# A hybrid Fourier and state-space layer on one core: the backward half of y and the C-B products are made earlier and kept in DRAM

## The chip, the cores and the metric

The kernel runs as one program on one core of a Trainium2 chip. The metric is the device time of an execution in microseconds; the time of a kernel is the median over its runs. In the text PE is TensorE, DVE is VectorE, ACT is ScalarE, POOL is GpSimd and SP is SyncE, whose queue issues every transfer of this kernel.

## What is computed

One layer of a mixer over 2048 latent tokens of width 1024, with a prefix of 256 context tokens. A combined projection feeds two groups: a Fourier group (512 channels) and an SSD group of 24 heads of 64 channels, four groups of six heads that share B and C of 128 states. The SSD group is scanned in both directions over chunks of 128 tokens; the latent scans start from the state that the context left. The part that the change is about, cut to its core:

```python
xbc = depthwise_conv_grid(xbc, conv_w, conv_b, rows, cols)     # SiLU inside; x, B and C
# per direction, per chunk c, group g, head r (ssd_chunked):
cb = einsum('bclgn,bcsgn->bgcls', cc, bc)                      # C-B product of a chunk, 128x128
y_diag = einsum('bgcls,bgrcls,bcsgrp->bclgrp', cb, lmat, xc)
states = einsum('bcsgn,bgrcs,bcsgrp->bcgrpn', bc, decay_states, xc)
new_state = decay * old_state + states                         # chunk after chunk
y_off = einsum('bclgn,bcgrpn,bgrcl->bclgrp', cc, prev_states, exp(a_cum))
# both directions, then
y = y_f + flip(y_b) + d_skip * xs
out = gated_rmsnorm(y * silu(zs))
```

The layer ends with the output projection, the residual and a final RMSNorm. All of it is in fp32. Products that need more than a single fp32r pass are made from a high part and a low part of each operand, in three matmuls (high x high, high x low, low x high); `split` makes the two parts, the high one by an ACT copy and the low one by a subtraction on DVE or POOL.

## The kernel before

The program is one list of stages. The framework orders the instructions of each engine when it builds the program, from a simulated timeline, with the order of the program text as priority; on the chip that order is fixed, and an instruction waits for its semaphores.

- **Up to 230 us**: adaLN, the norm of x, the projection of the Fourier channels.
- **conv** (230 to 765 us): 20 tiles of 128 channels (12 of x, 4 of B, 4 of C) in the order `CONV_ORDER`. For a tile PE projects four blocks of 512 tokens, ACT copies them into a padded image `img` (two buffers), and `finish` makes half an image at a time: one tap on ACT (L431), eight on DVE (L434) into `acc` (two buffers), then SiLU by ACT into `so` (L438). x and B tiles are transposed on PE in `to_tokens` (L414) and stored as `xtok_d` and `btok_d`; B and C are also stored untransposed in `bcT_d`, and C in two parts in `chl_d`. x and B tiles have the 256 context tokens beside it.
- **dt** (765 to 866 us): softplus of dt, cumulative sums, decays; `sml` holds the factors for the scan (ready with L546 of the second half), `sm_d`, `cum_d` and `q_d` keep others in DRAM. Two PE tiles of projections lie beside it.
- **scan** (870 to 1062 us): the context in both directions and the latent chunks 15 to 1 backwards. `scan_prep` loads x and B of a chunk, splits B (ACT, POOL), weighs x (POOL, L641) and splits it (ACT, DVE). `scan_mm`, four times a chunk, makes three matmuls and the new state from the old (L671 decay, L673 sum, both DVE) in the next of two buffers `hs`. The state before each chunk is stored in `hb_d`. Beside it runs the projection of zs, 40 blocks of 24 matmuls; `interleave(main, side, lead, speed)` mixes the two lists, here with a lead of 95 (scan work comes after the first 95 us of the main list by its written costs) and twice the even pace.
- **Fourier** (1065 to 1215 us): the rest of the Fourier group, and the last 12 blocks of zs. Its tables lie where the tiles of dt and scan were.
- **last stage** (1215 us to the end): 64 units, chunk by chunk forwards, four groups each, in six steps that overlap. `s1` makes the C-B product (L948), copies it, takes its diagonal (L953), makes `dsc` (L957: diagonal times backward dt, plus d_skip) and the decay matrix (L965 to L970). `s2` loads the state `hb` of the backward scan and makes y_off of both directions: `split` of `hf` (low part on DVE) and of `hb` (low part on POOL), three matmuls each (L1005 to L1007), a product with the decays (L1009), the term `xd` (six ACT instructions, L1012) and two sums on POOL (L1013, L1014). `s3` carries the forward state on, with a split of B on the spot. `s4` to `s6` are the diagonal part, the gated norm and the output projection (24 matmuls of 512 columns, L1105 to L1107).

Of the kernel before, what the change touches and what calls it, by code (L numbers as in the profile page):

```python
# [33 lines left out]
CONV_ORDER = [16, 0, 1, 2, 12, 17, 3, 4, 5, 13, 18, 6, 7, 8, 14, 19, 15, 9, 10, 11]  # L34
# [15 lines left out]
def mixer_layer(ctx: ExitStack, tc: tile.TileContext, A: dict, out: bass.AP, taps=None):  # L50
# [32 lines left out]
    btok_d = scratch("btok_d", [NALL, P, 4 * P])  # L83
    chl_d = scratch("chl_d", [NCH, P, G, 2, P], F32R)
    bcT_d = scratch("bcT_d", [NCH, P, G, 2, P])
# [5 lines left out]
    hb_d = scratch("hb_d", [NCH, P, DS])  # L91
# [21 lines left out]
    sc = const.tile([P, KT, 2], F32, name="sc")  # L113

# [281 lines left out]
    with ExitStack() as pc_:  # L396
# [14 lines left out]
        def to_tokens(src, ntile, dst):  # L411
# [5 lines left out]
            store(dst, tk[:, :ntile])  # L417

        def conv_tile(n, ci):
# [8 lines left out]
            def finish(half):  # L428
                r0 = 16 * half
                acc = cp.tile([P, 16, GRID_W], F32, name="acc", tag="acc")  # L430
# [5 lines left out]
                so = cp.tile([P, 8, P], F32, name="so", tag="so")  # L436
                sof = so[:].rearrange("p a b -> p (a b)")
                nc.scalar.activation(sof, acc[:].rearrange("p a b -> p (a b)"), AF.Silu, bias=convb[:, ci:ci + 1])  # L438
                c0 = 8 * half
                if kind == "x" or kind == "B":  # L440
                    dd = xtok_d if kind == "x" else btok_d
                    for q in range(2):
                        to_tokens(sof[:, 512 * q:512 * q + 512], 4,
                                  dd[c0 + 4 * q:c0 + 4 * q + 4, :, j * P:(j + 1) * P].rearrange("c p w -> p c w"))
                if kind != "x":
                    store(bcT_d[c0:c0 + 8, :, j, 0 if kind == "B" else 1, :].rearrange("c p w -> p c w"), so)
                if kind == "C":
                    parts = [cp.tile([P, 8, P], F32R, name=nm, tag=nm, bufs=1) for nm in ("sh", "sl")]
                    split(parts[0], parts[1], so, nc.gpsimd)
                    for i in range(2):  # L450
                        store(chl_d[c0:c0 + 8, :, j, i, :].rearrange("c p w -> p c w").bitcast(F32),
                              parts[i][:].bitcast(F32))
# [19 lines left out]
            so = cp.tile([P, CTX], F32, name="soc", tag="soc")  # L472
# [11 lines left out]
    ssdw = const_tile("ssdw", hfp)  # L484
    pp_ = ctx.enter_context(ExitStack())
    pers = pool("pers", stack=pp_)
    sml = pers.tile([P, NALL, 2, W2], F32, name="sml")

    zf_tile(2)
    pre1 = preload(LNEXP)  # L490
# [776 lines left out]
```

## Time and profile before

| | us |
|---|---|
| median of 3 runs | 1980.51 (1978.22 to 1981.74) |
| the profiled execution, its own time | 1983.29 |
| its span, first to last instruction | 1981.4 |
| PE busy | 1848.8 (93%) |
| DVE busy | 1447.8 (73%) |
| ACT busy | 882.0 (45%) |
| POOL busy | 822.4 (42%) |
| DMA traffic | 253.75 MB, 128 GB/s on average |

The mean granted TensorE clock is 0.972 of full speed. How to read the views: busy time is the time in which an engine has an instruction running, and a matmul's end is modelled, so PE's share is high wherever matmuls follow each other. In a row of a tile stand the line, the engine, what is written and read, the count, the shortest, median and longest duration in ns, and the first and last start. A row of waits names who waited for whom, the total, the times and the longest. The chain of waits goes back from the last instruction, at each step to what released it.

### The profile page before, as it was taken

The numbers are of one execution on the slowest core, as the hardware profiler recorded it, in microseconds if no ns is written. First come the engines' busy times: TensorE is split into PE (matmuls) and PEld (weight loads), VectorE is DVE, ScalarE is ACT, GpSimd is POOL, SyncE is SP. The second block draws the span as 40 slices with busy tenths as digits, with TensorE's granted clock in tenths as the row PEclk, the third lists the DMA queues.
The fourth block names the chain that finished last, engine by engine and source line by source line (L and its number), as shares of the span: only waits on it lengthen the run. The fifth ranks groups of instructions, "written<-read, shape, count | busy, mean of one in ns | idle before, by whom it ended". The sixth has DMA issues, their size and how long they took to land.

```text
span 1981.4 us, 27052 instructions
## 1 busy us (share of the span) xinstructions
PE 1848.8 (93%) x9136; PEld 1510.2 (76%) x9136; DVE 1447.8 (73%) x2082; ACT 882.0 (45%) x2008; POOL 822.4 (42%) x635
## 2 busy tenths in 40 slices
PE   6999999999999999999889997889989999899997
PEld 2799988878888888888767786767777777677775
DVE  3742398998988986329995137988988887888873
ACT  2631144344444443443233335655555555555553
POOL 1321021111101110136662226777777767776742
PEclk8999999999999999999999998899999999999998
DMA  7332132322423423356777456543343343333320
GB/s 265 142 95 77 34 107 66 106 88 74 115 59 91 128 62 111 110 167 233 251 261 261 149 179 196 177 135 116 111 122 108 113 122 120 113 108 116 114 89 36
DMA packets 233468, 253.75 MB, mean 128 GB/s; under 512 B 23313, under 2 KB 194417, under 8 KB 232818
## 3 DMA queue, kind: packets, MB, share of 16 engines
q1 hardware_dynamic: 233330, 252.03, 41.0%
q8 instruction: 73, 1.20, 0.3%
q14 instruction: 65, 0.53, 0.1%
HBM read 165.94 MB, written 86.02 MB: 127 GB/s over the span
## 4 chain that ended last, share of the span: by engine, by line
PE 54%; DVE 30%; DMA 5%; ACT 4%; issue 4%; POOL 1%; SPq 1%; DVEq 0%; ACTq 0%; POOLq 0%
DVE acc L434 10%; PE pj L170 8%; PE pj L169 8%; PE pj L171 8%; PE po L1105 4%; PE po L1106 4%; PE po L1107 4%; DMA hb_d<-hs 2%; DVE w L970 2%; DVE xl L72 2%; PE pj L381 2%; PE pj L380 2%; PE pj L379 2%; PE py L1046 1%; DVE hs L671 1%
## 5 line engine op out<-in xcount | busy, mean ns | idle before, releaser
L434 DVE SCALAR_TENSOR_TENSOR acc<-img,c_convw,acc 128x1024 f32<-128x1024 f32 x320 | 464.2, 1458 | 58.8 <-ACT acc L431 48.9
L170 PE MATMUL pj<-hl,wh 128*128 128x512 f32 x1152 | 453.2, 393 | 0.0
L169 PE MATMUL pj<-hh,wh 128*128 128x512 f32 x1152 | 452.0, 396 | 1.2 <-DVE hs L673 1.2
L171 PE MATMUL pj<-hh,wl 128*128 128x512 f32 x1152 | 452.4, 393 | 0.0
L72 POOL TENSOR_TENSOR wl<-raw,wh 128x1024 fp32r<-128x1024 f32 x48 | 122.3, 2548 | 591.5 <-ACT wh L68 568.0
L171 PEld LDWEIGHTS pj<-hh,wl 128*128 128x128 f32 x1152 | 217.3, 189 | 45.1 <-issue 0.2
L169 PEld LDWEIGHTS pj<-hh,wh 128*128 128x128 f32 x1152 | 218.2, 189 | 43.7 <-DVE hs L673 1.5
L170 PEld LDWEIGHTS pj<-hl,wh 128*128 128x128 f32 x1152 | 217.7, 189 | 42.0 <-issue 1.8
L1105 PE MATMUL po<-hl,mh 128*128 128x512 f32 x384 | 160.1, 417 | 21.2 <-ACT mh L68 19.7
L1106 PE MATMUL po<-hh,mh 128*128 128x512 f32 x384 | 155.2, 404 | 0.4 <-DVE hh L729 0.4
L1107 PE MATMUL po<-hl,ml 128*128 128x512 f32 x384 | 146.1, 403 | 0.6 <-POOL ml L72 0.6
L1012 ACT ACTIVATE xd<-xg,dsc 128x64 f32<-128x64 f32 x384 | 98.7, 336 | 36.9 <-DVE dsc L957 34.1
L965 PE MATMUL parg<-rt,lt 128*128 128x384 f32 x256 | 96.8, 390 | 17.1 <-DVE parg L967 10.9
L1105 PEld LDWEIGHTS po<-hl,mh 128*128 128x128 f32 x384 | 74.2, 193 | 42.8 <-ACT mh L68 25.8
L438 ACT ACTIVATE so<-acc,c_convb 128x1024 f32<-128x1024 f32 x40 | 46.1, 1153 | 129.9 <-DVE acc L434 129.9
L72 POOL TENSOR_TENSOR ml<-gt,mh 128x384 fp32r<-128x384 f32 x64 | 68.4, 1069 | 84.4 <-ACT mh L68 81.9
L1013 POOL TENSOR_TENSOR us<-us,xd 128x384 f32<-128x384 f32 x64 | 66.1, 1033 | 77.9 <-ACT xd L1012 77.7
L68 ACT ACTIVATE mh<-gt 128x384 fp32r<-128x384 f32 x64 | 33.4, 522 | 120.2 <-DVE gt L1071 117.1
L72 POOL TENSOR_TENSOR sl<-hb,sh 128x384 fp32r<-128x384 f32 x64 | 81.5, 1273 | 11.9 <-ACT sh L68 11.8
L641 POOL TENSOR_TENSOR xt<-xt,sml 128x768 f32<-128x768 f32 x38 | 66.9, 1780 | 46.7 <-DMA xt<-xtok_d 24.6
L1106 PEld LDWEIGHTS po<-hh,mh 128*128 128x128 f32 x384 | 74.3, 194 | 14.7 <-DVE hh L729 0.9
L1107 PEld LDWEIGHTS po<-hl,ml 128*128 128x128 f32 x384 | 71.7, 191 | 17.9 <-POOL ml L72 4.3
(390 smaller groups left out, 4158.7 us busy)
## 6 DMA issues: line engine op xcount, KB each, us to landing
raw<-in_win SPq DMA_DIRECT2D x48, 512.0 KB
xt<-xtok_d SPq DMA_DIRECT2D x19, 768.0 KB
xtok_d<-tk SPq DMA_DIRECT2D x48, 256.0 KB
zsT_d<-ev SPq DMA_DIRECT2D x48, 256.0 KB
hb_d<-hs SPq DMA_DIRECT2D x16, 768.0 KB
hb<-hb_d SPq DMA_DIRECT2D x64, 192.0 KB
zs<-zsT_d SPq DMA_DIRECT2D x64, 192.0 KB
xg<-xtok_d SPq DMA_DIRECT2D x64, 192.0 KB
```

The costliest lines, as they stand in the source:

```text
L72: (lo_engine or nc.vector).tensor_tensor(out=lo, in0=src, in1=hi.bitcast(F32), op=ALU.subtract)
L169: mm(po, wh[:, k], a, start=(k == 0), stop=False)
L170: mm(po, wh[:, k], b, start=False, stop=False)
L171: mm(po, wl[:, k], a, start=False, stop=(k == KT - 1))
L434: nc.vector.scalar_tensor_tensor(out=acc, in0=im[:, r0 + dy:r0 + dy + 16, dx:dx + GRID_W], scalar=tap(t), in1=acc, op0=ALU.mult, op1=ALU.add)
L641: nc.gpsimd.tensor_tensor(out=xq, in0=xq, in1=wd, op=ALU.mult)
L965: mm(po, l[:, dr], r[:, cols], start=True, stop=True)
L1012: nc.scalar.activation(xd[:, h], xg[:, h], AF.Copy, scale=d["dsc"][:, h:h + 1])
L1013: nc.gpsimd.tensor_tensor(out=us, in0=us, in1=xd, op=ALU.add)
L1105: mm(po, a, wh[:, i], start=(g == 0 and q == 0), stop=False)
L1106: mm(po, a, wl[:, i], start=False, stop=False)
L1107: mm(po, b, wh[:, i], start=False, stop=(g == 3 and q == 3))
```

## The change

1. **conv**: SiLU is made in place in `acc` (`so` and `soc` go; C has its own two buffers `cacc`). B is split in two parts once, after its transposition (high part ACT, low part POOL), and stored as `bhl_d` in place of `btok_d`. The 64 C-B products are made here (`cb_products`) from C's and B's halves and stored in `cb_d`; `bcT_d` goes. Their diagonals `cbd` come from a product with the identity on POOL and a reduction on DVE. In `CONV_ORDER` each B tile comes right behind its C tile.
2. **dt**: `ecb` (backward exp of the cumulative sums) and `dsc` for all chunks.
3. **scan**: works by single groups instead of chunks. `scan_off` makes the backward y_off, adds `xd` and stores the sum in `yb_d`, in place of the state `hb_d`. The state is kept in place (`hbk`, `hf`); its decay moves from DVE to POOL. x is weighed into a tile of its own. The list has no lead and runs at the even pace; loads run two units ahead.
4. **last stage**: loads `cb`, `yb` and the split B; the C-B product, its copy and diagonal, `dsc`, the backward y_off, `xd`, one of the two POOL sums and the split of B go. The low part of `hf` moves from DVE to POOL.

The diff, cut to its core:

```diff
-CONV_ORDER = [16, 0, 1, 2, 12, 17, 3, 4, 5, 13, 18, 6, 7, 8, 14, 19, 15, 9, 10, 11]
+CONV_ORDER = [16, 12, 0, 1, 2, 17, 13, 3, 4, 5, 18, 14, 6, 7, 8, 19, 15, 9, 10, 11]
...
+        def hl_store(dst, parts, c0, n, j):
+            for i in range(2):
+                store(dst[c0:c0 + n, :, j, i, :].rearrange("c p w -> p c w").bitcast(F32),
+                      parts[i][:, :n].bitcast(F32))
+
+        def b_tokens(src, j, c0, n):
+            parts = hl_tiles()
+            for q in range(0, n, 4):
+                m = min(4, n - q)
+                split(*(t[:, q:q + m] for t in parts), to_tokens(src[:, P * q:P * (q + m)], m), nc.gpsimd)
+            hl_store(bhl_d, parts, c0, n, j)
+
+        def cb_products(bt, ct, j, c0):
+            for q in range(0, 8, 4):
+                pt = tr_psum([P, 4, P])
+                for i in range(q, q + 4):
+                    mm(pt[:, i - q], bt[:, i * P:(i + 1) * P], ct[:, i * P:(i + 1) * P], start=True, stop=True)
+                tk = cp.tile([P, 4, P], F32, name="tk", tag="tk")
+                copy(tk, pt)
+                store(cb_d[c0 + q:c0 + q + 4, :, j, :].rearrange("c p w -> p c w"), tk)
+                dg = cp.tile([P, 4, P], F32, name="dg", tag="dg", bufs=1)
+                nc.gpsimd.tensor_tensor(out=dg, in0=tk, in1=ident[:].unsqueeze(1).broadcast_to([P, 4, P]), op=ALU.mult)
+                nc.vector.tensor_reduce(out=cbd[:, c0 + q:c0 + q + 4, j], in_=dg, axis=AX.X, op=ALU.add)
...
-                acc = cp.tile([P, 16, GRID_W], F32, name="acc", tag="acc")
+                acc = cp.tile([P, 16, GRID_W], F32, name="acc", tag="cacc" if kind == "C" else "acc")
...
-                nc.scalar.activation(sof, acc[:].rearrange("p a b -> p (a b)"), AF.Silu, bias=convb[:, ci:ci + 1])
+                nc.scalar.activation(sof, sof, AF.Silu, bias=convb[:, ci:ci + 1])
...
+                elif kind == "B":
+                    b_tokens(sof, j, c0, 8)
+                    cb_products(sof, cso[half], j, c0)
...
+            nc.gpsimd.tensor_copy(out=ecb[:, cl], in_=ecum[:, :nl, H:])
+            dv = dsc[:, cl]
+            nc.vector.tensor_tensor(out=dv, in0=dtt[:, :nl, H:]..., in1=cbd[:, cl]..., op=ALU.mult)
+            nc.vector.tensor_tensor(out=dv, in0=dv, in1=dsk[:]..., op=ALU.add)
...
+        def scan_prep(dr, c, g):
             def go():
+                gs = slice(g * GW, (g + 1) * GW)
+                d = st[dr, c, g] = {}
+                xt = d["x"] = sp.tile([P, HG, 64], F32, name="xt3", tag="xt", bufs=4)
+                load(xt[:].rearrange("p h w -> p (h w)"), xtok_d[c, :, gs])
+                if dr == 1 and c < NCH:
+                    d["c"] = sp.tile([P, 2, P], F32R, name="cc3", tag="cc", bufs=3)
+                    load(d["c"][:].bitcast(F32), chl_d[c, :, g].bitcast(F32))
+                if (dr, c) == (1, 0):
+                    return
+                d["b"] = sp.tile([P, 2, P], F32R, name="bb3", tag="bb", bufs=3)
+                load(d["b"][:].bitcast(F32), bhl_d[c, :, g].bitcast(F32))
+                xw = sp.tile([P, HG, 64], F32, name="xw3", tag="xw")
...
+                nc.gpsimd.tensor_tensor(out=xw, in0=xt, in1=wd, op=ALU.mult)
+                d["xh"], d["xl"] = (sp.tile([P, GW], F32R, name=t + "3", tag=t, bufs=3) for t in ("xh", "xl"))
+                split(d["xh"], d["xl"], xw[:].rearrange("p h w -> p (h w)"))
...
+        def scan_off(c, g):
+            def go():
+                gs = slice(g * GW, (g + 1) * GW)
+                d = st[1, c, g]
+                sh, sl = (sp.tile([P, GW], F32R, name=t + "3", tag=t) for t in ("sh", "sl"))
+                split(sh, sl, hbk[:, gs])
+                po = main_psum()[:, :GW]
+                mm(po, d["c"][:, 0], sh, start=True, stop=False)
+                mm(po, d["c"][:, 0], sl, start=False, stop=False)
+                mm(po, d["c"][:, 1], sh, start=False, stop=True)
+                yb, xd = (sp.tile([P, HG, 64], F32, name=t, tag=t) for t in ("yb3", "xd3"))
+                for h in range(HG):
+                    nc.scalar.activation(xd[:, h], d["x"][:, h], AF.Copy, scale=dsc[:, c, g, h:h + 1])
+                ec = ecb[:, c, g * HG:(g + 1) * HG].unsqueeze(2).broadcast_to([P, HG, 64])
+                nc.vector.tensor_tensor(out=yb, in0=po.rearrange("p (h w) -> p h w", w=64), in1=ec, op=ALU.mult)
+                nc.gpsimd.tensor_tensor(out=yb, in0=yb, in1=xd, op=ALU.add)
+                store(yb_d[c, :, gs], yb[:].rearrange("p h w -> p (h w)"))
...
+        def scan_mm(dr, c, g):
...
+                nc.gpsimd.tensor_tensor(out=h3, in0=h3, in1=dec, op=ALU.mult)
+                nc.vector.tensor_tensor(out=hv, in0=hv, in1=pst, op=ALU.add)
...
-        interleave(zs_ops([(7, range(4))] + [(i, (0, 1, 2)) for i in range(8, 20)]), side, 95, 2, True)
+        interleave(zs_ops([(7, range(4))] + [(i, (0, 1, 2)) for i in range(8, 20)]), side, 0, 1, True)
...
-            split(sh, sl, hsrc, (nc.vector, nc.gpsimd)[dr])
...
-        nc.gpsimd.tensor_tensor(out=us, in0=us, in1=xd, op=ALU.add)
-        nc.gpsimd.tensor_tensor(out=ts, in0=ts, in1=us, op=ALU.add)
+        split(sh, sl, hf[:, gs], nc.gpsimd)
+        mm(po, d["chl"][:, 0], sh, start=True, stop=False)
+        mm(po, d["chl"][:, 0], sl, start=False, stop=False)
+        mm(po, d["chl"][:, 1], sh, start=False, stop=True)
+        ec = d["sml"][:, 2, g * HG:(g + 1) * HG].unsqueeze(2).broadcast_to([P, HG, 64])
+        nc.vector.tensor_tensor(out=ts, in0=po, in1=ec, op=ALU.mult)
+        nc.gpsimd.tensor_tensor(out=ts, in0=ts, in1=yb, op=ALU.add)
...
-        bh, bl = (wa.tile([P, P], F32R, name=t, tag=t, bufs=1) for t in ("bh4", "bl4"))
-        split(bh, bl, d["b"], nc.vector)
+        bh, bl = d["b"][:, 0], d["b"][:, 1]
```

178 lines of the change are left out of this document (71 added, 107 removed).

## The prediction

> **What bounds the kernel now.** I read the busy times by stage first, then the chain of waits stage by stage, then single tiles. The stages (columns: stretch, its length, then PE, weight loads, DVE, ACT and POOL busy, clock, DMA share, GB/s) are conv, scan and the last stage with its 64 units; dt and Fourier lie between:
>
> ```profile
> 230.00:765.00 535.00, 526.67 (x2625) 444.69 (x2624) 475.16 (x354) 221.87 (x315) 70.31 (x28) 0.99 0.30 87
> ...
> 866.00:1065.00 199.00, 182.98 (x818) 152.00 (x817) 166.35 (x200) 63.31 (x90) 120.52 (x65) 0.97 0.71 238
> ...
> 1215.00:1982.00 767.00, 684.94 (x3569) 540.53 (x3567) 628.62 (x1210) 422.30 (x1292) 523.70 (x470) 0.95 0.38 116
> ```
>
> PE looks full everywhere, but matmuls overlap in the record, so this alone is no bound. DVE is busy for 89% of conv, 84% of the scan and 82% of the last stage. The chain of waits for conv, the scan and most of the last stage (the view cuts its long line):
>
> ```profile
> by line: DVE acc L434 35.9%; PE pj L169 16.5%; PE pj L170 16.5%; PE pj L171 16.4%; PE ptr L414 4.5%; ACT so L438 1.7%; PE pc L170 1.6%; PE pc L169 1.6%; PE pc L171 1.6%; ACT acc L431 1.1%; issue 0.8%; DVE accc L470 0.6%; ACT img L68 0.6%; A
> ...
> by line: DMA hb_d<-hs 17.5%; DVE xl L72 16.2%; DVE hs L671 14.7%; DVE hs L673 9.4%; DVE gate L686 8.1%; issue 7.7%; PE pj L170 6.1%; PE pj L171 6.0%; PE pj L169 5.9%; DVE hs L668 1.7%; DVE hf L671 1.1%; PE ptr L689 1.0%; DVE hf L673 0.8%; P
> ...
> by line: PE po L1105 11.1%; PE po L1106 10.6%; PE po L1107 10.5%; issue 6.4%; DVE w L970 4.5%; PE py L1046 3.9%; DVE parg L967 3.8%; DVE sl L72 3.1%; DVE rs L1069 3.0%; DVE bl L72 3.0%; ACT xd L1012 2.9%; DVE gt L1071 2.7%; DVE hf L1037 2.5
> ```
>
> Conv is shared between PE and the DVE taps, so both are near critical. The scan hangs on DVE and on a store. The last stage is a mixture in which PE has a third. Next, single tiles (min/median/max ns), and one collision, out of the chain and out of POOL's timeline:
>
> ```profile
> L434 DVE SCALAR_TENSOR_TENSOR acc<-img,c_convw,acc x320: 1270/1285/3506, 238.4 to 763.4; 128x1024 f32<-128x1024 f32 x160
> L72 POOL TENSOR_TENSOR wl<-raw,wh x48: 2366/2540/3117, 21.4 to 1169.8; 128x1024 fp32r<-128x1024 f32 x48
> L1009 DVE TENSOR_TENSOR us<-pyo,sml x64: 537/545/559, 1217.0 to 1926.3; 128x384 f32<-128x384 f32 x64
> L72 DVE TENSOR_TENSOR sl<-hf,sh x64: 541/549/2451, 1205.7 to 1913.7; 128x384 fp32r<-128x384 f32 x64
> L72 POOL TENSOR_TENSOR sl<-hb,sh x64: 988/1250/1742, 1208.8 to 1917.8; 128x384 fp32r<-128x384 f32 x64
> ...
> 398.33 3.35 DVE acc L434
> ...
> 398.19 2.40 POOL L72 TENSOR_TENSOR sl<-so,sh 128x1024 fp32r<-128x1024 f32 x1 [10.10 <-ACT sh L68]
> ```
>
> POOL runs from 398.19 to 400.59; the tap started beside it ends at 401.68, 1.09 us after POOL, where it needs 1.27 alone. So the two took turns but for 0.18 us. A DVE split with two SBUF inputs (sl from hf) ranges from 541 to 2451 ns, while a product with a PSUM input (us) stays within 537 to 559 in the same stage, beside the same POOL work. I therefore add POOL's instructions and DVE's two-SBUF-input instructions into one sum, called the shared path, and take 0.18 us off each DVE one.
>
> The Trainium skill, page "SBUF — State Buffer", section "SBUF: two separate sides", says that the pair of ports shared by VectorE and GpSimd is locked for the whole instruction and that the loser blocks fully. The collision above agrees but for its 0.18 us; what whole durations would make of the scan is rival (4).
>
> **The conv stage.** Prices of what it gets:
>
> ```profile
> L1056 DVE TENSOR_REDUCE s<-sq x64: 579/598/608, 1229.5 to 1956.3; 128x128 f32<-128x384 f32 x64
> DVE acc L434 <- ACT acc L431: 48.9, 17, 6.8
> ...
> 1512.84 0.49 PE L948 MATMUL pcb<-bc 128*128 128x128 f32 x2
> 1513.16 0.38 PE L1049 MATMUL py<-c_ident,ts 128*128 128x128 f32 x2
> ```
>
> The split of B adds 16 low parts of 512 columns and 4 of 256 on POOL (sl of hb takes 0.99 for 384, so 1.32 and 0.66: 24 us), with as many ACT copies. The C-B products add 64 matmuls (0.32 us to the next start, 20 us), 16 ACT copies, 16 POOL products with the identity (21 us) and 16 DVE reductions (0.58 for 384 columns, so 0.77: 12 us). Stores of bcT and btok go, those of bhl and cb come: 36 on SP become 40, at nothing, since the stage moves 87 GB/s. ACT is busy 222 of 535 us and hides its copies. So DVE gets 12 us, and behind 45 us of POOL work up to 40 us of turns, 52 in all; PE gets 20. The lower end is 14, if DVE stays covered by PE and a product costs a third less; the upper is 60, if DVE also stands before a reduction until POOL's identity product is done, with the next taps behind it. The waits for L431 (48.9 us) show that DVE has little reserve, but only 4 of the 20 tiles carry the load and img has two buffers. I take **+38**, nearer to DVE's price. SiLU in place keeps an acc buffer until its transposes are done; its next user comes a half tile, some 13 us, later, so nothing. If that cover is gone, L431 waits on ACT with DVE behind it. ecb and dsc are six small operations in the dt stage, where DVE is mostly idle: 0.
>
> **The scan stage.** Its start, end and prices:
>
> ```profile
> 852.94 0.61 DVE L546 TENSOR_TENSOR sml<-sml,smx 128x432 f32<-128x432 f32 x1
> L673 DVE TENSOR_TENSOR hs<-hs,ptr x32: 536/541/555, 915.6 to 1062.1; 128x384 f32<-128x384 f32 x32
> L641 POOL TENSOR_TENSOR xt<-xt,sml x38: 1468/1786/2191, 870.1 to 1044.9; 128x768 f32<-128x768 f32 x38
> L72 POOL TENSOR_TENSOR bl<-bt,bh x19: 1289/1641/2008, 873.0 to 1051.5; 128x512 fp32r<-128x512 f32 x19
> L72 DVE TENSOR_TENSOR xl<-xt,xh x38: 942/1122/3161, 872.5 to 1055.1; 128x768 fp32r<-128x768 f32 x38
> L671 DVE TENSOR_TENSOR hs<-hs,sml x64: 543/558/2233, 905.0 to 1058.9; 128x384 f32<-128x384 f32 x64
> L686 DVE SCALAR_TENSOR_TENSOR gate<-ev,sc,gate x16: 736/1307/2469, 891.1 to 1042.9; 128x512 f32<-128x512 f32 x16
> L1025 POOL TENSOR_TENSOR xw<-xg,sml x60: 823/836/1550, 1207.7 to 1879.1; 128x384 f32<-128x384 f32 x60
> L1036 POOL TENSOR_TENSOR hf<-hf,sml x60: 822/872/1547, 1209.8 to 1875.1; 128x384 f32<-128x384 f32 x60
> L1013 POOL TENSOR_TENSOR us<-us,xd x64: 996/1012/1726, 1219.7 to 1942.5; 128x384 f32<-128x384 f32 x64
> L1012 ACT ACTIVATE xd<-xg,dsc 128x64 f32<-128x64 f32 x384 | 98.7, 336 | 36.9 <-DVE dsc L957 34.1 <-DMA lt<-q_d 0.8 <-POOL xl L72 0.7
> L63 SPq DMA_DIRECT2D hb_d<-hs x16: 319/320/539, 924.5 to 1062.7; - x16
> ```
>
> Before, 870 to 1062, by minima: on POOL xt 38 x 1.468, bl 19 x 1.289 and about 8 wl x 2.37; on DVE xl 38 x 0.942, the decay of hs and hf 68 x 0.543, gate 16 x 0.736: 184 us. Less 122 x 0.18 this is 162 us on the shared path in 192, 0.84 full.
>
> After: on POOL xw 76 x 0.823, the decay 68 x 0.822, yb plus xd 64 x 0.996, wl 19: 201 us; on DVE xl 76 x 0.541, sl 64 x 0.541, gate 12: 88. That is 289, less 156 x 0.18: 261 us. The yb products and the state sums read PSUM and run beside it. At 0.84 full the scan takes 311 us, wholly full 261. The hb_d store, 17.5% of the stage's chain (35 us of 199), goes, and without it 162 us would have filled all of 157; so I take a value between, 0.92: 284 us. Beside it lie ACT (99 us of xd and 64 sh splits on top of 63) and PE. SP gets 276 transfers (76 xt, 72 B, 64 C, 64 yb) instead of 54, at 0.32 us 71 us more of issuing within 284: hidden. The wait that is added is SP's for POOL before each yb store; behind it stand the loads two units on and the next weights. The start is set by sml (ready at 853.6): without the lead 856 instead of 870. The end is 1140 instead of 1062: **+78** (+55 to +105). The Fourier stage follows, because its tables lie where sml and the scan's tiles were; PE, free for part of the scan, may do a few of its zs blocks early: **-10** (0 to -50).
>
> **The last stage.** Its period and PE's spacing:
>
> ```profile
> L1052 DVE SCALAR_TENSOR_TENSOR gt<-py,zs x64: 537/545/559, 1226.9 to 1955.1; 128x384 f32<-128x384 f32 x64
> 1506.21 0.34 PE L1005 MATMUL pyo<-sh,chl 128*128 128x384 f32 x1
> 1506.39 0.34 PE L1006 MATMUL pyo<-sl,chl 128*128 128x384 f32 x1
> 1508.08 0.39 PE L1105 MATMUL po<-hl,mh 128*128 128x512 f32 x1
> 1508.32 0.39 PE L1106 MATMUL po<-hh,mh 128*128 128x512 f32 x1
> ```
>
> A unit takes (1955.1-1226.9)/63 = 11.56 us. Out of it go PE's pcb and three pyo (0.32 + 3 x 0.18 = 0.86), DVE's us, dsc, diagonal and bl, ACT's cb, bh, one sh and six xd, POOL's sum of us and xd (1.0). The split sl of hf moves from DVE to POOL, where it takes the place of that of hb. PE's large matmuls need 24 x 0.24 + 13 x 0.18 = 8.1 us; with the small ones, about one us (estimated from pcb), 9.1 now and 8.2 after. In the chain above sl, bl and xd have 9.0% of the time, and us, dsc, the diagonal, pcb and pyo, by their lengths, some 6% more: 15% off gives 9.8 us. The shared path loses POOL's 1.0 and most of DVE's three splits, which shortens the turns of w, rs and gt: I take 9.6, so 1.95 x 63 = **-123**. The ends are 10.5 (PE as full as now, 8.2 of 10.5), -65, and 9.1 (PE 90% full), -155. SP issues as many loads a unit as before: 0.
>
> Sum: +38+78-10-123 = -17 on the profiled execution's 1983.3 (span 1981.4), 1966; the median of the runs is 2.8 lower, so 1964.
>
> **The rivals.** (1) Slower: SP stands before each yb store, the loads two units on come late, and a unit of the scan loses 0.67 us: 51 more, 2015. For it: stores already hold 17.5% of that chain. Against: a slice is a quarter of hb_d's. It decides once the scan takes over 301 us. (2) PE uses its free time in the scan for most of the 12 zs blocks of the Fourier stage (24 x 0.24 each, 69 us): 40 us more off, 1924. Against: the order on an engine is fixed at build. (3) The last stage waits as it does now and gains 65: 2022. (4) Work is moved and not saved: the shared path counts whole durations, 289 us at the 184/192 of before, so 302, end 1158, 18 more: 1982, no change. Against: the 0.18 us above.
>
> **How the numbers follow.** Forecast 0.44 (its own range 1935 to 2000), (1) 0.25, (2) 0.14, (3) 0.10, (4) 0.07. The range reaches from (2) past (1) and (3), 1918 to 2028, which leaves out some 2 in 10 of their spread. Within 0.2% (4 us), about what a measurement of this kernel can tell from no change, lie a part of the forecast and most of (4): 0.10. Faster is three quarters of the forecast and (2), 0.47; slower 0.43.
>
> **What would show it.** gt's period near 9.6 us; a scan from 856 to 1140 with POOL busy for three quarters of it; DVE near 520 us busy in conv, where it was 475; the decay of the backward state gone from DVE's rows. The forecast is wrong if the scan ends later than 17 us past its 1140 beyond conv's shift, or if gt's period stays above 10.

## The result and the profile after

The changed kernel takes 1996.16 us (median of 4 runs, 1995.1 to 1998.23) against 1980.09 us for the kernel before: a ratio of 1.0083, 95% interval 1.0065 to 1.0100. It is 0.8% slower, where the forecast was 0.8% faster. The profiled execution took 1995.1 us, its span 1993.2.

The busy times of the changed kernel by stage, in the columns of the prediction's first table (conv, dt, scan, last stage), and behind them dt and scan of the kernel before:

```profile
230.00:802.00 572.00, 544.89 (x2746) 459.56 (x2744) 505.10 (x369) 238.30 (x350) 144.27 (x64) 0.99 0.29 82
802.00:891.00 89.00, 55.19 (x252) 43.08 (x250) 36.20 (x57) 27.02 (x42) 5.94 (x4) 0.79 0.38 109
891.00:1190.00 299.00, 283.66 (x1264) 238.20 (x1264) 202.53 (x294) 189.20 (x572) 230.69 (x220) 0.94 0.72 216
1340.00:1994.00 654.00, 599.58 (x3247) 478.96 (x3247) 498.75 (x834) 286.32 (x721) 448.28 (x410) 0.96 0.45 136
```

```profile
765.00:870.00 105.00, 105.00 (x502) 86.99 (x501) 33.30 (x48) 45.88 (x63) 11.98 (x5) 1.00 0.45 128
870.00:1062.00 192.00, 175.98 (x787) 146.19 (x786) 165.80 (x199) 62.12 (x88) 120.52 (x65) 0.97 0.71 237
```

Two things stand out. In dt TensorE was busy for all of 105 us with 502 matmuls; now it is busy for 55 of 89 us with 252, at a granted clock of 0.79. In the scan it was busy for 176 of 192 us with 787 matmuls; now it has 1264 and is busy for 284 of 299 us. Of the 477 matmuls more, 192 are new there (three of y_off for each of 64 units), and 250 are those that dt no longer has. The stage's engines that the forecast looked at, DVE and POOL, are busy for 0.68 and 0.77 of it.

The single tiles that date the stages in the changed kernel (min/median/max ns, first start to last start; the line numbers are those of the changed kernel):

```profile
L470 DVE SCALAR_TENSOR_TENSOR acc<-img,c_convw,acc x320: 1269/1285/3352, 238.2 to 801.0; 128x1024 f32<-128x1024 f32 x160
L579 DVE TENSOR_TENSOR sml<-sml,smx x2: 607/608/610, 847.7 to 879.6; 128x432 f32<-128x432 f32 x2
L686 POOL TENSOR_TENSOR xw<-xt,sml x76: 822/830/1382, 891.6 to 1161.9; 128x384 f32<-128x384 f32 x76
L725 POOL TENSOR_TENSOR hbk<-hbk,sml x64: 819/832/1156, 909.2 to 1172.9; 128x384 f32<-128x384 f32 x64
L706 POOL TENSOR_TENSOR yb<-yb,xd x64: 1000/1288/1482, 925.3 to 1189.4; 128x384 f32<-128x384 f32 x64
L1088 DVE SCALAR_TENSOR_TENSOR gt<-py,zs x64: 540/550/560, 1353.4 to 1967.2; 128x384 f32<-128x384 f32 x64
L1107 DVE TENSOR_TENSOR gt<-gt,rs x64: 542/884/1539, 1363.4 to 1975.5; 128x384 f32<-128x384 f32 x64
```

Read one below the other with the rows of the kernel before, they give the balance. The last tap starts at 801.0 instead of 763.4 (+37.6). The scan ends with the last sum of yb, 1189.4 and its one us, instead of 1062.6 (+128, so +90 beyond conv). The first gt starts at 1353.4 instead of 1226.9 (+126.5), so the Fourier stage between takes 163 us as it took 164. A unit of the last stage takes (1967.2 - 1353.4) / 63 = 9.74 us instead of 11.56, so the 63 periods between the first and the last gt give back 114 us. The last gt is 12.1 us later than before, and so is the span (+11.8).

The scan starts when x arrives and not when sml is ready, which is at 880.2: SP issues the first load of x at 888.90, behind dt's last stores, and POOL waits for it (the row in POOL's timeline, with its wait in brackets):

```profile
891.63 0.83 POOL L686 TENSOR_TENSOR xw<-xt,sml 128x384 f32<-128x384 f32 x1 [13.33 <-DMA xt<-xtok_d]
```

The chain of waits of the changed kernel, for the scan and for the last stage (the view cuts its long line):

```profile
by line: PE pj L172 17.0%; PE pj L170 16.9%; PE pj L171 16.8%; issue 3.9%; DMA xt<-xtok_d 3.5%; PE ptr L717 3.4%; POOL yb L706 3.3%; PE ptr L716 3.3%; PE ptr L718 3.2%; PE pj L698 2.8%; DMA ev<-in_wada_g 2.8%; POOL xw L686 2.8%; PE pj L699 
...
by line: PE po L1143 14.0%; PE po L1142 13.8%; PE po L1141 13.7%; PE py L1082 5.7%; issue 4.9%; PE parg L1008 4.2%; PE py L1085 3.2%; DMA wo<-in_wout 2.7%; DMA xg<-xtok_d 2.4%; DVE gt L1107 1.8%; PE pn L1098 1.6%; DVE w L1013 1.6%; DVE parg
```

In the kernel before, the scan hung on DVE and a store; now the three matmuls of the zs projection (L170 to L172) hold half of its chain. In the last stage TensorE's output matmuls, the first of the chain before too, went from a third of it to over 41%, and DVE's lines fell behind.

### The profile page after: what moved, and what is told of

Read it like the earlier page. It is cut to its first block, busy times and chain, and to the rows that moved or that the text cites. A ratio compares the mean times of both kernels' runs of the same rounds, so it can differ in the third digit from the quotient of the medians.

```text
span 1993.2 us, 27660 instructions
## 1 busy us (share of the span) xinstructions
PE 1835.8 (92%) x9136; PEld 1507.1 (76%) x9136; DVE 1382.5 (69%) x1820; ACT 868.2 (44%) x1932; POOL 918.8 (46%) x760
## 4 chain that ended last, share of the span: by engine, by line
PE 37%; DVE 7%; DMA 6%; POOL 3%; ACT 2%; issue 2%; SPq 1%; DVEq 0%; ACTq 0%; POOLq 0%
PE po L1143 5%; PE po L1142 5%; PE po L1141 5%; PE pj L170 4%; PE pj L172 4%; PE pj L171 4%; PE py L1082 2%; PE parg L1008 1%; DMA wo<-in_wout 1%; PE py L1085 1%; DMA xg<-xtok_d 1%; PE ptr L849 1%; SPq L63 1%; DVE gt L1107 1%; PE pn L1098 1%
## 5 line engine op out<-in xcount | busy, mean ns | idle before, releaser
L470 DVE SCALAR_TENSOR_TENSOR acc<-img,c_convw,acc 128x1024 f32<-128x1024 f32 x320 | 485.6, 1524 | 49.2 <-ACT acc L467 39.6
L172 PE MATMUL pj<-hh,wl 128*128 128x512 f32 x1152 | 455.4, 395 | 0.0
L170 PE MATMUL pj<-hh,wh 128*128 128x512 f32 x1152 | 453.5, 398 | 0.0
L172 PEld LDWEIGHTS pj<-hh,wl 128*128 128x128 f32 x1152 | 218.5, 190 | 45.9 <-issue 0.5
L170 PEld LDWEIGHTS pj<-hh,wh 128*128 128x128 f32 x1152 | 219.4, 190 | 42.0 <-issue 1.8
L703 ACT ACTIVATE xd<-xt,dsc 128x64 f32<-128x64 f32 x384 | 101.3, 336 | 75.9 <-POOL yb L706 69.8
L473 ACT ACTIVATE acc<-acc,c_convb 128x1024 f32<-128x1024 f32 x40 | 46.1, 1152 | 160.4 <-DVE acc L470 160.4
L1012 ACT ACTIVATE w<-parg 128x384 f32<-128x384 f32 x128 | 62.3, 487 | 110.0 <-DVE parg L1010 109.6
L1013 DVE TENSOR_TENSOR w<-w,cb 128x768 f32<-128x768 f32 x64 | 85.9, 1342 | 13.1 <-ACT w L1012 12.3
L68 ACT ACTIVATE xh<-xw 128x384 fp32r<-128x384 f32 x136 | 70.2, 517 | 56.7 <-POOL xw L686 25.1
L686 POOL TENSOR_TENSOR xw<-xt,sml 128x384 f32<-128x384 f32 x76 | 68.4, 901 | 52.8 <-DVE xl L72 32.5
L1051 POOL TENSOR_TENSOR ts<-ts,yb 128x384 f32<-128x384 f32 x64 | 73.8, 1154 | 40.8 <-issue 18.3
L1010 DVE COPY_PREDICATED parg<-msk,parg 128x384 f32<-128x384 uint8 x128 | 70.8, 553 | 30.3 <-PE parg L1008 30.2
L68 ACT ACTIVATE tk<-ptr 128x512 f32<-128x512 f32 (+1 forms) x96 | 51.3, 556 | 88.7 <-PE ptr L415 50.6
```

The source lines that it names most:

```text
L68: return nc.scalar.activation(dst, src, AF.Copy).ins
L170: mm(po, wh[:, k], a, start=(k == 0), stop=False)
L172: mm(po, wl[:, k], a, start=False, stop=(k == KT - 1))
L470: nc.vector.scalar_tensor_tensor(out=acc, in0=im[:, r0 + dy:r0 + dy + 16, dx:dx + GRID_W], scalar=tap(t), in1=acc, op0=ALU.mult, op1=ALU.add)
L703: nc.scalar.activation(xd[:, h], d["x"][:, h], AF.Copy, scale=dsc[:, c, g, h:h + 1])
L1013: nc.vector.tensor_tensor(out=w, in0=w, in1=cb[:].unsqueeze(1).broadcast_to([P, HG, P]), op=ALU.mult)
```

## The experiments

Two theories stood at first. "PE": the lead before the first scan step (95 us of projection work, removed by the change) kept TensorE busy during dt; without it that work falls into the scan, and TensorE sets the scan's length. "Shared path": the POOL instructions and DVE's two-SBUF-input instructions, taken in turns, set it. Ratios are to the kernel before on the same chip, with 95% intervals; the changed kernel's is 1.0083. Most intervals reach 0.002 to each side, 4 us; the times inside a run come from one profiled execution.

**The lead put back into the changed kernel.**

```
-        interleave(zs_ops(...), side, 0, 1, True)
+        interleave(zs_ops(...), side, 95, 2, True)
```

> The changed kernel with the scan list's lead of 95 and pace of 2 of before. Theory PE (without the lead the scan's steps stand ahead of zs blocks in PE's order while sml is not ready, so PE loses some 42 us in the dt stage, and PE, not the shared path, then sets the scan's end): PE is full again between the end of conv and the scan, the scan of 299 us becomes 255 to 280, the total falls by 25 to 45 us, to 1951 to 1971. Theory shared path (POOL and DVE's two-input instructions set the scan's length, as in the prediction): the scan starts some 15 us later and stays 285 to 300 long; total 1996 to 2010.

Measured: 1996.78 us, 1.0084 (1.0064 to 1.0105), no change, as "shared path" expected. The sums of yb run from 961.7 to 1193.8 and the weighting starts at 909.1: the scan takes 286 us instead of 299, but starts 17 us later. "PE" alone, which expected 1951 to 1971, is refuted.

**A lead of 60 at a pace of 1.45.**

```
-        interleave(zs_ops(...), side, 0, 1, True)
+        interleave(zs_ops(...), side, 60, 1.45, True)
```

> The changed kernel with a lead of 60 and a pace of 1.45: just the zs blocks that fit beside the dt stage come first. Theory PE: as good as the lead of 95 or better by up to 10 us, since the scan's work is spread over more zs blocks; 1945 to 1970. Theory shared path: 1990 to 2000, as the changed kernel.

Measured: 1990.8 us, 1.0060 (1.0039 to 1.0080); the time is what "shared path" expected, the interval overlaps that of the changed kernel, and the profiled execution, at 1983.62 us, was the shortest of six. From 802 to 912 us TensorE now does 486 matmuls, where it did 252 in dt. The scan runs from 912.2 to 1180.9, 269 us. Its tile row, and one window of it beside the same window of the changed kernel (in this order):

```profile
L706 POOL TENSOR_TENSOR yb<-yb,xd x64: 989/1322/1468, 944.6 to 1179.9; 128x384 f32<-128x384 f32 x64
```

```profile
1100.00:1150.00 50.00, 45.63 (x207) 36.80 (x206) 42.12 (x57) 35.12 (x113) 44.26 (x43) 1.00 0.75 231
```

```profile
1100.00:1150.00 50.00, 50.00 (x235) 42.74 (x234) 33.60 (x49) 33.84 (x104) 39.58 (x36) 1.00 0.73 222
```

With this lead TensorE has 207 matmuls in 50 us and room, while DVE and POOL go from 33.6 and 39.6 us to 42.1 and 44.3: the limit has passed from TensorE to the shared path. Summed as in the prediction, by minima (yb's adds 64 x 0.99, and the rest as above), the path holds some 260 us of work in these 269 (0.97 full), and 268 in the changed kernel's 299 (0.90; three more low parts of weights fall into it).

**The lead taken from the kernel before, and its double pace with it.**

```
-        interleave(zs_ops(...), side, 95, 2, True)
+        interleave(zs_ops(...), side, 0, 1, True)
```

> The kernel before with no lead and the even pace (0, 1), nothing else. Theory PE: the same loss without the rest of the change: PE's need fills only some 0.6 of the dt stage instead of all of it, some 20 us of the 40 lost are made up by PE's slack in the scan (0.89 full), total 1990 to 2010. Theory shared path: the scan can start earlier and runs at its own length, total 1970 to 1980.

Measured: 2035.67 us, 1.0276 (1.0253 to 1.0299), the largest effect of all runs, and larger than expected. Its dt and scan, by window, and the last state sums:

```profile
764.00:845.00 81.00, 33.00 (x132) 23.93 (x131) 33.01 (x50) 20.26 (x35) 7.54 (x5) 0.62 0.35 104
845.00:1110.00 265.00, 259.60 (x1177) 219.06 (x1176) 173.30 (x199) 74.71 (x106) 120.77 (x66) 0.99 0.59 192
```

```profile
L673 DVE TENSOR_TENSOR hs<-hs,ptr x32: 537/546/555, 888.8 to 1109.9; 128x384 f32<-128x384 f32 x32
```

The scan starts some 30 us earlier (xt at 839.8 instead of 870.1) and ends 48 us later. TensorE is busy for 33 of 81 us in dt, and then for 98% of the scan with 1177 matmuls in place of 787. So in a kernel whose scan has room on the shared path, the lead and its pace together are worth 56 us, and the early start does not make up for them.

**More buffers for the stores of yb.** This was rival (1).

```
-                yb, xd = (sp.tile(..., tag=t) for t in ("yb3", "xd3"))
+                yb, xd = (sp.tile(..., tag=t, bufs=4) for t in ("yb3", "xd3"))
```

> The changed kernel with four buffers for yb and xd in the scan instead of two. Rival (1) of the prediction (stores of yb, and SP standing before them, set the pace): the scan gets 15 to 50 us shorter. Theory PE and theory shared path: within 5 us of the changed kernel, although ACT's 70 us of waits of xd for POOL's yb shrink.

Measured: 1997.56 us, 1.0084 (1.0057 to 1.0111). The buffers make no difference that shows.

**The sum of yb moved off POOL.** The product stays in PSUM, and DVE adds xd from there.

```
-                nc.vector.tensor_tensor(out=yb, in0=po..., in1=ec, op=ALU.mult)
-                nc.gpsimd.tensor_tensor(out=yb, in0=yb, in1=xd, op=ALU.add)
+                p3 = po.rearrange(...)
+                nc.vector.tensor_tensor(out=p3, in0=p3, in1=ec, op=ALU.mult)
+                nc.vector.tensor_tensor(out=yb, in0=p3, in1=xd, op=ALU.add)
```

> In the scan the sum of the two halves of the backward y is moved from POOL (64 adds of 1182 ns) to DVE: the product stays in PSUM and DVE adds the other half from there. The lead stays 0. Theory 'two limits': in the changed kernel both the path that POOL and DVE share (254 us of work in 299) and PE (271 us) are near the scan's length; taking some 48 us from the path leaves PE as the limit, so the scan shortens only to 280-288 us and the time is 1980 to 1987 us. Theory 'path alone': 206 us of work at 0.85 give a scan of 242 us and a time of 1936 to 1945 us. Theory 'PE alone': no change, 1992 to 1998 us.

Measured: 1990.91 us, 1.0045 (1.0027 to 1.0063): between "two limits" (1980 to 1987) and "PE alone" (1992 to 1998), nearer to the second, and far from "path alone". The scan runs from 893.0 to 1185.5, 292 us; "two limits" expected 280 to 288. POOL is now busy for half of each window and TensorE for nearly all of it, so TensorE held the scan, and the path gave little:

```profile
1050.00:1100.00 50.00, 50.00 (x237) 43.29 (x236) 35.31 (x64) 33.26 (x104) 24.71 (x26) 1.00 0.74 227
```

**The sum of yb on DVE, and the lead of 60.**

> As the run before this one (the add on DVE from PSUM), and with the lead of 60 us and speed 1.45 as in the run with lead 60. Theory 'two limits': PE has then 215 us of work left for the scan and the path 200 us; at 0.9 to 0.95 the scan takes 226 to 240 us instead of 269, and the time is 1948 to 1962 us, so that the two edits together bring far more than the sum of each alone (6 and 12 us). Theory 'path alone': the same as the run with lead 0 but for the start, 1936 to 1945 us in both. Theory 'PE alone': as lead 60 by itself, 1986 to 1992 us.

Measured: 1984.81 us, 1.0011 (0.9994 to 1.0029). All three expectations miss, "PE alone" by only a microsecond: the scan still takes 266 us (912.2 to 1178.3), though TensorE and POOL have room: between 1000 and 1150 TensorE is busy for at most 45.9 of 50 us, POOL for 28.6. The waits of this run between 920 and 1170 name a third limit (who waited for whom: us in total, times, longest):

```profile
POOL xw L686 <- DMA xt<-xtok_d: 50.1, 35, 4.3
ACT xh L68 <- POOL xw L686: 42.9, 40, 3.8
```

POOL's weighting waits for x out of DRAM. In the changed kernel the same wait, over the same window, is a tenth of it:

```profile
POOL xw L686 <- DMA xt<-xtok_d: 5.8, 5, 2.6
```

There, it seems, the other two limits hold everything back first; the next runs test this.

**Loads four units ahead, with both edits above, and two more buffers each for x, B and C.**

```
+        FAR = 4
...
+            if n + FAR < len(seq):
+                side.append((0.0, scan_load(*seq[n + FAR])))
```

> The run with the add on DVE and lead 60, and the scan's loads (x, C, B) issued four units ahead of their use in place of two, with two more buffers each; the weighting and split still two ahead. In that run POOL's weighting waited 50 us for x in 35 places. Theory 'loads': SP issues in order, so the loads stand behind the stores of y that wait for their product, and two units ahead is too late; four ahead removes most of the 50 us, the scan takes 225 to 245 us in place of 266, and the time is 1945 to 1965 us. Rival 'bandwidth': the queues move 227 GB/s at 0.74 to 0.8 of the DMA engines' time and can't bring x sooner however early it is asked for; the scan keeps 260 to 270 us and the time is 1980 to 1988 us.

Measured: 1967.67 us, 0.9935 (0.9914 to 0.9955): faster than both kernels. The wait for x falls, and the scan ends 18 us earlier, after 248 us:

```profile
POOL xw L694 <- DMA xt<-xtok_d: 10.7, 6, 2.3
```

```profile
L715 DVE TENSOR_TENSOR yb<-pj,xd x64: 540/546/559, 944.6 to 1159.7; 128x384 f32<-128x384 f32 x64
```

So x was asked for too late rather than moved too slowly: between 1000 and 1150 the queues now bring 246 to 259 GB/s, where they brought 212 to 249. The scan of 248 us and the time are 3 us above what "loads" expected, and 12 below "bandwidth".

**Earlier loads alone.**

> The changed kernel with the scan's loads issued four units ahead and nothing else. Theory 'several limits': PE is busy 50 of 50 us in each window from 1000 on, so earlier loads alone bring at most 5 us: 1990 to 1998 us. Rival 'loads alone': the scan of the changed kernel is late because of its loads, and it gains 15 to 30 us: 1966 to 1981 us.

Measured: 1992.72 us, 1.0051 (1.0028 to 1.0074). The scan ends at 1187.9 instead of 1190.4. As "several limits" expected, the loads alone bring little.

**Earlier loads and the lead, with the sum on POOL.**

> The changed kernel with lead 60 (speed 1.45) and loads four units ahead; the add of the backward y stays on POOL. It completes the set of three edits. Theory 'three limits, each hiding the others': with PE and the loads relieved, the shared path with its 248 us of work is what is left, at 0.92 to 0.95 full 261 to 269 us of scan, 1982 to 1990 us. Rival 'the add does not matter': the scan is as short as with all three edits (248 us), 1966 to 1973 us.

Measured: 1986.26 us, 1.0028 (1.0010 to 1.0046); the scan runs from 913.7 to 1182.5, 269 us, inside what "three limits" expected. From the run with all three edits (1967.67 us) it differs in the place of the sum alone, and that is worth 21 us of scan. The shared path is what is left, and it is nearly full again:

```profile
1100.00:1150.00 50.00, 47.07 (x214) 39.44 (x213) 43.15 (x57) 34.81 (x111) 47.14 (x43) 0.97 0.76 231
```

POOL is busy for 47 of 50 us. The ends of the scan, side by side, show how the three edits hide each other: none 1190.4; loads 1187.9; sum on DVE 1185.5; lead 1180.9; lead and loads 1182.5; lead and sum 1178.3; all three 1160.3. Single edits bring 3 to 10 us, all three 30; the sum with earlier loads and no lead was not run. How fine are these figures? In the changed kernel and four other runs whose scan is the same but for buffers, the last sum of yb starts 387.2 to 389.2 us after the last tap of conv. Counted so, the loads alone bring 2 us, hardly outside that spread, the sum 5, the lead 8 and all three 29. By this measure the three together clearly bring more than the sum of the single edits, 15. By the ratios of whole times they bring 6, 8 and 5 alone and 29 together, each with some 5 us to either side, which by itself would hardly show it.

**Half of the change: the products, the diagonal and the split of B in conv, the backward half of y in the last stage as before.** States are kept in DRAM and the lead is 95. The edit is shown against the kernel before, cut to its core.

```
-            split(bh, bl, bt, nc.gpsimd)
+            load(b2, bhl_d[c])
...
         scan_mm, the stores of hb_d and the lead as in the kernel before
...
+        load(dsc4, dsc_d[c, :, g])
         both halves of y in s2 as in the kernel before
```

> Half of the change alone: C-B products, their diagonal and the split of B are made in the conv stage and kept in DRAM as in the changed kernel, but the backward half of y stays in the last stage, with the states kept in DRAM, the lead of 95 and the scan's instructions as in the kernel before (less the split of B). Expected: conv +38 as in the changed kernel; scan 182 to 192 us (PE need 171 at 0.9 as before, POOL freed of 32 us of splits); last stage less some 45 us, since 99 us of DVE work leave it (diagonal 17 + 5, its scaling 43, split of B 34) and DVE was busy 610 of 728. Sum 1965 to 1985 us. If the last stage is bound by the path alone (the split of B only, 64 x 0.4), it gains 20 to 28 and the time is 1985 to 1998 us.

Measured: 1973.02 us, 0.9954 (0.9939 to 0.9970), faster than the kernel before.

```profile
L710 DVE TENSOR_TENSOR hs<-hs,ptr x32: 540/544/555, 954.8 to 1098.5; 128x384 f32<-128x384 f32 x32
L1076 DVE SCALAR_TENSOR_TENSOR gt<-py,zs x64: 540/546/558, 1259.8 to 1944.3; 128x384 f32<-128x384 f32 x64
```

The scan ends 36 us later than before, which is conv's growth. A unit takes (1944.3 - 1259.8) / 63 = 10.87 us instead of 11.56, so the last stage gives back 44. Beside the changed kernel this splits the change: the other half, which moves the backward half of y and takes away the lead, puts the first gt 94 us later (1353.4 - 1259.8) and gives back 71 in the last stage (10.87 - 9.74, 63 times). That half loses 23 us, and the half of this run gains 9 (1982.20 - 1973.02). The sum lies inside what was expected.

**Conv: without the diagonal, its factor set to 1.**

```
-                nc.gpsimd.tensor_tensor(out=dg, in0=tk, in1=ident..., op=ALU.mult)
-                nc.vector.tensor_reduce(out=cbd[...], in_=dg, axis=AX.X, op=ALU.add)
```

> The diagonal of the C-B products (16 POOL multiplies and 16 DVE reductions in the conv stage) is left out; the factor that it makes is set to 1, so the backward half of y lacks that factor. All else as in the changed kernel. Theory 'diagonal': the 37 us that the conv stage grew come mostly from these instructions, 11 us of reductions in DVE's queue and some 16 x 1 us in which POOL's multiply keeps DVE's taps waiting, so the last tap ends 20 to 30 us earlier (771 to 781) and the time is 1966 to 1976 us. Rival 'PE order': the growth comes from what stands in PE's queue (64 C-B matmuls, 12 us, and transposes that wait for the split and the copies), so the last tap stays within 6 us of 801 and the time is 1990 to 1997 us.

Measured: 1988.09 us, 1.0032 (1.0016 to 1.0047). The last tap starts at 790.2, 11 us earlier, between the two expectations. That is the length of the 16 reductions (0.68 us each), but the match is partly chance: DVE's 17.0 us of waits for POOL's product also go, and its taps get 7.6 us shorter (444.1 to 436.5), while its waits for ACT's tap grow by 20 us (31.8 to 51.4). The run prices the diagonal as a whole and does not split it.

**Conv: without the diagonal and the C-B products; a slice of C is stored in their place.**

```
-                    mm(pt[:, i - q], bt[...], ct[...], start=True, stop=True)
-                copy(tk, pt)
+                tk = ct[:, q * P:(q + 4) * P]...
```

> As the run without the diagonal, and also without the 64 C-B matmuls and their 16 copies out of PSUM in the conv stage; a slice of C is stored where the product was, so y is another. The run without the diagonal ended conv at 791.5 and took 1988 us. Theory 'PE': the matmuls (12 us of PE's need) and their place in PE's order, behind a Silu, carry the rest, so conv ends at 770 to 783 and the time is 1968 to 1981 us. Rival 'B split': the rest comes from the 20 splits of B on POOL (39 us busy) in turns with DVE's taps; conv ends at 787 to 792 and the time is 1984 to 1991 us.

Measured: 1974.08 us, 0.9960 (0.9940 to 0.9981). The taps of the run without the diagonal and of this one:

```profile
L468 DVE SCALAR_TENSOR_TENSOR acc<-img,c_convw,acc x320: 1268/1285/3437, 237.6 to 790.2; 128x1024 f32<-128x1024 f32 x160
```

```profile
L464 DVE SCALAR_TENSOR_TENSOR acc<-img,c_convw,acc x320: 1270/1285/3349, 237.5 to 778.3; 128x1024 f32<-128x1024 f32 x160
```

Another 12 us go with the 64 matmuls and 16 copies. So conv's 37.6 us are 11 for the diagonal, 12 for the products, and 15 for what is left: the split of B, the SiLU in place and the order of the tiles.

**Conv: the old order of tiles.**

```
-CONV_ORDER = [16, 12, 0, 1, 2, 17, 13, 3, 4, 5, 18, 14, 6, 7, 8, 19, 15, 9, 10, 11]
+CONV_ORDER = [16, 0, 1, 2, 12, 17, 3, 4, 5, 13, 18, 6, 7, 8, 14, 19, 15, 9, 10, 11]
```

> The changed kernel with the conv stage's tiles in the order of the kernel before (each B tile two or three tiles behind its C tile, not right behind it). Theory 'order': two tiles in a row whose products and transposes wait for the same Silu leave PE waiting (51 us of waits of transposes on Silu against 16 before); with the old order the last tap ends 10 to 25 us earlier and the time is 1972 to 1986 us. Rival 'instructions': the growth of conv comes from the added instructions alone and the last tap stays within 5 us of 801: 1991 to 1999 us.

Measured: 1996.72 us, 1.0079 (1.0058 to 1.0099), with the last tap at 796.2, as "instructions" expected. In nine runs with the conv stage of the changed kernel the last tap starts at 799.6 to 801.1, so the order is worth some 3 to 5 us in conv; the whole time does not show it.

> The half of the change that was 0.5% faster than the kernel before (products and split in conv, backward half of y in the last stage), with the conv stage's old order of tiles. If the order costs what 'order' says, 1950 to 1965 us; if it costs nothing, 1970 to 1977 us.

This is the half of the change once more, with the old order of tiles. Measured: 1967.91 us, 0.9923 (0.9898 to 0.9948). The interval overlaps that of the run without the order (0.9939 to 0.9970), so a difference between the two is not shown.

**All edits of the scan, and the old order.**

> The changed kernel with lead 60, the add on DVE from PSUM, loads four units ahead and the conv stage's old order of tiles, which ended conv 4 us earlier. Expected: 4 us less than the run without the order, 1960 to 1968 us, 0.7 to 1.1% under the kernel before.

Measured: 1963.25 us, 0.9901 (0.9873 to 0.9929), the lowest median of all versions, 1% under the kernel before; its interval overlaps those of the run without the order and of the half of the change with it. Conv ends 3 us earlier than in the run without the order, and the scan's sums end at 1156.6 instead of 1160.3.

## Why the prediction was wrong

The sum was -17 us against the kernel before's profiled execution; it came out at +12. No single term carries the difference of 29: three of four were each some 10 us too good.

- **Conv, +38: right, at +37.6, and right in its bounds; its split was not.** The forecast gave DVE 12 us of reductions and up to 40 of turns with POOL, took a value between 14 and 60, and that it met the measured one is luck. DVE's taps took 485.6 us in all instead of 464.2, so the turns that were added came to some 21. The runs show 11 for the diagonal as a whole, and 12 for the C-B products, which stood there as PE's 20. DVE is busy for 505 us, not 520. The 15 us that are left were not taken apart.
- **Scan, +78: +90, and here the failing step lies.** The start came out right by luck: 856 and conv's 38 make 894, and it came at 891.6. But the forecast had it set by sml, which was ready 11 us before, and the first load of x came later than it. The duration was 299 instead of 284. The sentence that failed is "Beside it lie ACT ... and PE", together with the removal of the lead counted as a gain of 14 us in the start alone: TensorE's need in the scan was put at nothing, without a sum. The lead was what let TensorE do 502 matmuls during dt. Without it TensorE did 252 there, carried the rest into the scan, got 192 new ones beside, and was full in it: its 1264 matmuls, at the 235 in 50 us of the full window shown above, need 269 us (an estimate). The run with a lead of 60 has the path at 0.97 full, better than the forecast's 0.92, and a scan of 269; the kernel before without its lead and pace is 56 us slower. The rows for this stood in the profile: 105 of 105 us busy in dt. The forecast's own sign, a scan more than 17 us late beyond conv's shift, was too wide to catch it: the scan was 12 us late.
- **The shared path as the scan's limit: right, but as one of three.** Counted as the forecast counted it, it fits the two runs with a lead of 60 in which POOL keeps the sum, at 269 us in each, and moving the sum shortens the second of them to 248. (With the lead of 95 the sums of yb begin only at 961.7, and the scan takes 286.) Its count was a little off: 12 low parts of weights and 12 gate instructions fell into the scan, not 8 and 16, and SP had 284 transfers there, not 276. The path is why putting the lead back brings 10 us at most: the path is right behind TensorE, and the loads are right behind the path.
- **Rival (1) was half of it.** More buffers for yb change nothing. But loads that were asked for two units ahead did come late once the other limits were lifted, 50 us of waits, and four units ahead only 11.
- **Fourier, -10: -1.** TensorE did nothing early, and rival (2) falls with it. That TensorE was full in the scan is not the whole reason: with the lead of 60 it was busy for 45.6 us of 50, and from the end of the scan to the first gt it still took 162 us (1180.9 to 1342.6). The order fixed at build, which the forecast set against rival (2), fits; no run tests it.
- **Last stage, -123: -114.** The period is 9.74, not 9.6, inside the bound of 10. TensorE's share of its chain has grown, and gt's scaling takes 884 ns in the median where it took 546 in the kernel before; turns of POOL and DVE would explain this, but no run separates them. Rival (3), 65, is far off.
- **Rival (4), whole durations:** its scan of 302 us is near the measured 299, but for another reason. TensorE was busy for 284 of these 299 us, and with the lead of 60 the same kinds of POOL and DVE instructions, 287 us in whole durations, fitted into 269. So each of the 152 DVE instructions among them overlapped POOL's by at least 0.12 us on average; the 0.18 us of the forecast fit that, and were not tested by themselves. The Trainium skill, page "SBUF — State Buffer", section "SBUF: two separate sides", has the shared pair held for the whole instruction. Taken for whole recorded durations, that is not borne out by this kernel.
- **The range** (1918 to 2028) held the time.

## What to carry to other kernels

A lead that fills one engine during another stage is work, not delay: before you price its removal, count what that engine does in the stage (here 502 matmuls in 105 us) and where it will have to do it. Work moved into a stage must be set against each resource of that stage by itself, engines, shared ports and the depth of its loads, because the longest alone shows in the profile, and an edit that lifts one uncovers the next: here three edits brought 3, 5 and 10 us of scan alone and 30 together. And split a change before you judge it: one half of this one was faster than the kernel before, and the other half, which lost the lead too, took more in the scan than it gave back later.

## What the runs showed of the hardware

TensorE did not come back at full speed after it had been idle. The changed kernel in steps of 10 us, from the end of dt into the scan (the eighth number is the granted clock):

```profile
842.00:852.00 10.00, 4.17 (x19) 2.07 (x17) 4.16 (x9) 5.77 (x8) 0.36 (x1) 0.70 0.64 183
852.00:862.00 10.00, 5.13 (x23) 4.13 (x22) 1.93 (x4) 1.72 (x4) 0.00 (x0) 0.50 0.21 57
862.00:872.00 10.00, 0.55 (x3) 0.38 (x2) 7.12 (x10) 2.41 (x3) 0.00 (x0) 0.50 0.00 0
872.00:882.00 10.00, 4.83 (x17) 2.71 (x17) 5.83 (x12) 4.34 (x7) 0.33 (x1) 0.76 0.31 82
882.00:892.00 10.00, 0.51 (x3) 0.23 (x3) 1.78 (x3) 1.08 (x3) 0.37 (x1) 0.58 0.47 122
892.00:902.00 10.00, 7.31 (x16) 4.30 (x17) 6.07 (x11) 3.14 (x6) 8.32 (x10) 0.50 0.85 260
902.00:912.00 10.00, 7.96 (x19) 4.72 (x19) 7.58 (x13) 3.65 (x7) 8.52 (x10) 0.50 0.74 223
912.00:922.00 10.00, 8.41 (x22) 6.44 (x23) 6.60 (x11) 6.27 (x20) 7.91 (x10) 0.54 0.45 135
922.00:932.00 10.00, 8.73 (x42) 7.37 (x41) 6.88 (x12) 6.35 (x19) 6.66 (x7) 1.00 0.55 169
```

From 852 to 892, where TensorE does little, the clock stands between 0.50 and 0.76. From 892 to 922 it is still at about one half, though TensorE is busy for 73% to 84% of the time, and the matmuls in 10 us double when it returns to 1.00. The 57 matmuls of these 30 us kept TensorE busy for 24 us; at the pace of the next row (42 in 8.73 us) they would have taken some 12, an estimate that takes them for alike. A lead of 60 does not avoid this. There TensorE was full until 900, and after 10 us of little work the same half clock lasted to 940:

```profile
900.00:910.00 10.00, 3.56 (x18) 2.54 (x16) 2.12 (x4) 1.55 (x3) 0.00 (x0) 0.80 0.60 168
910.00:920.00 10.00, 5.58 (x13) 3.66 (x14) 5.91 (x9) 2.62 (x5) 6.86 (x8) 0.50 0.83 261
...
930.00:940.00 10.00, 7.63 (x20) 5.81 (x20) 6.54 (x11) 5.67 (x18) 7.49 (x10) 0.50 0.56 175
940.00:950.00 10.00, 10.00 (x48) 8.63 (x48) 8.16 (x12) 5.79 (x15) 8.68 (x9) 0.99 0.56 162
```

In the kernel before, TensorE is busy for all of 840 to 910 us, and the clock stays at 1.00. The Trainium skill, page "TensorE: Matmul & The Clock Gate", section "Part 1: The HAM clock gate (the "warmup" mystery)", states that the clock is halved when TensorE has been idle and comes back after about 3.4 us of sustained activity. The half agrees; here it took 30 us from the scan's start, with gaps between the matmuls.

A DVE sum whose one input lies in PSUM took 546 ns in the median and never over 559 beside POOL's work, where POOL's sum of the same tiles took 1288 in the changed kernel. In the runs with this sum the product before it writes its result back into PSUM. That move freed POOL of 64 sums at the price of 64 short DVE instructions.
